# Delta rule inverse: substitution on 16-wide blocks only, larger blocks joined on TensorE in turn

## The chip, the cores and the metric

One Trainium2 chip, one NeuronCore of it. The metric is the device time of one execution in microseconds (us). All arithmetic is in 32-bit floats; the large projections split each operand into two rounded parts and take three products.

## The reference, cut to what matters

Two small model blocks run one after the other on a sequence of 512 tokens of width 1024. The second block's first mixer is a gated delta rule with 16 value heads of width 128, which this change touches:

```python
L = jnp.where(strict, jnp.einsum('bhncd,bhnsd->bhncs', kb, k) * decay, 0.0)
eye = jnp.eye(CHUNK, dtype=q.dtype)
T = lax.linalg.triangular_solve(eye + L, jnp.broadcast_to(eye, L.shape),
                                left_side=True, lower=True, unit_diagonal=True)
u = T @ vb
w = T @ (kb * jnp.exp(g)[..., None])
...
def step(state, inp):
    v_new = u_n - jnp.einsum('bhcd,bhde->bhce', w_n, state)
    o = (jnp.einsum('bhcd,bhde->bhce', q_n, state)
         + jnp.einsum('bhcs,bhse->bhce', a_n, v_new))
    state = state * gl_n[..., None, None] + jnp.einsum('bhcd,bhce->bhde', k_n, v_new)
```

T is the inverse of a unit lower triangular matrix, one for each head and chunk of tokens. The scan over chunks needs T of a chunk before it can go on.

## The kernel before

The kernel is one program written through a layer that traces every operation in program order, finds the dependencies, allots buffers of named tiles, and then orders each engine's instructions itself by a planner's cost model; it sets all semaphores. Each engine then works through its own list in that order. So the order of the trace is the planner's and not that of the source, and taking operations away may reorder others.

The delta rule is the function `gdn`. It works in chunks of 128 tokens, four of them, and on pairs of value heads (gi = 0 to 7) which share a key head; a pair has 8 matrices (2 heads x 4 chunks), numbered n.

- `stage_a(gi)` projects q and k (L1083), convolves and normalises them, makes the products k k and q k (L1099), multiplies them with masks and decays into `Am` (L1120, L1121, on VectorE) and `At` (L1122, on GpSimd, as are the products `qd` of L1126), and inverts.
- The inverse starts from the 32x32 diagonal blocks, 4 per matrix, 32 in all. They go through DRAM (`ad`, L1131 and L1135) into `ai`, so that each partition holds one whole block, four copies of it; partition group s then solves eight of its 32 columns, `ui`. L1138 loads unit columns. Substitution is row by row: the loop of L1140 to L1144 solves the two 16-wide halves of the block at once in 15 steps of a product and a sum; L1146 to L1149 take what the first half gives to the second; L1150 to L1153 solve the second half's rows for the first half's columns, 15 steps more. Each step needs the one before.
- The result goes back through DRAM (`ud`, L1156 and L1162) into `uc`, 32 rows of each block in 32 partitions; `tcp` is its transpose by 32x32 blocks (L1164).
- The join: 32-wide blocks are joined to 64 (L1177 to L1191) and 64 to 128 (L1192 to L1198) by two matrix products each, over the PSUM tile `mg`, of which there is one buffer. The first loop goes through the two 64-wide halves m one after the other, each with its eight matrices in a row, so that eight products in a row use the same 32x32 part of the array. ScalarE copies results to `z32`, `tz` and the result `U`.
- `stage_v` and `stage_z` project values and gates; `stage_b` is the scan over chunks, which reads `U` in L1243; `stage_g` normalises and gates; `stage_o` projects out, its sums evicted by VectorE in L1292.

The loop of L1297 emits, for each gi, `stage_v(gi + 1)`, `stage_a(gi + 2)`, `stage_b(gi)`, `stage_z(gi)`, `stage_g(gi)` and `stage_o(gi - 1)`, so a pair's inverse is emitted two iterations ahead of its use. Projections are in the helper `mm3` (L145 to L147); their weights are fetched on SP's queue (L138), rounded by ScalarE (L139) and their rests taken by VectorE (L140), in three buffers; their sums go to three PSUM banks `acc`.

Of the kernel before, what the change touches and what calls it, by code (L numbers as in the profile page):

```python
# [12 lines left out]
AF = mybir.ActivationFunctionType  # L13
ALU = mybir.AluOpType
AX = mybir.AxisListType
# [4 lines left out]
D, S, DFF, KT, P = 1024, 512, 2816, 8, 128  # L20
# [415 lines left out]
def fdims(t, off, *dims):  # L436

    return bass.AP(tensor=t.tensor, offset=t.offset + off, ap=[list(t.ap[0])] + [list(d) for d in dims])
# [528 lines left out]
def gdn(self, feed0, gate, tail):  # L967
    nc, tc, A = self.nc, self.tc, self.A
    with tc.tile_pool(name="gd", bufs=1) as gd, tc.tile_pool(name="gdd", bufs=1, space=bass.MemoryType.DRAM) as dr:
        def T(name, shape=(P, S), dtype=F32, bufs=None):  # L970
            return gd.tile(list(shape), dtype, name=name, bufs=bufs)
# [102 lines left out]
        def stage_a(gi):  # L1074
# [3 lines left out]
            for u in range(2):  # L1078
# [5 lines left out]
                x = T(f"x{u}", bufs=2 + u)  # L1084
# [3 lines left out]
            rb, r, pk = norms(qk, 1.0, "sa", gi < 2)  # L1088
# [5 lines left out]
            q, k = qk  # L1094
# [17 lines left out]
            Am, At = T("Am", (P, 8, P), bufs=2), T("At", (P, 8, P), bufs=2)  # L1112
            for a in range(2):
# [5 lines left out]
                m = Am[:, a * 4:(a + 1) * 4, :]  # L1119
# [6 lines left out]
                nc.gpsimd.tensor_mul(qd[:, a], q, gbc[:, a])  # L1126


            ad = dr.tile([8, 4, 32, 32], F32, name="ad", bufs=2)
            for b in range(4):  # L1130
                nc.sync.dma_start(ad[:, b].rearrange("n j i -> j n i"), Am[32 * b:32 * b + 32, :, 32 * b:32 * b + 32])  # L1131
            ai = T("big", (P, 32, 32), bufs=3)
# [4 lines left out]
            ui = T("ui", (P, 8, 32), bufs=2)  # L1137
            nc.sync.dma_start(ui, A["gdn_eye"])  # L1138
            mt = T("mt", (P, 2, 4, 16), bufs=2)
            for t in range(1, 16):  # L1140
# [2 lines left out]
                                     fdims(ai, t, (528, 2), (0, nq), (32, t + 1)))  # L1143
                nc.vector.tensor_reduce(fdims(ui, t, (144, 2), (32, nq), (1, 1)), mt[:, :, :nq, :t + 1], axis=AX.X,  # L1144
                                        op=ALU.add, negate=True)
            for v in range(2):  # L1146
                x = T("ix").rearrange("p (q i j) -> p q i j", q=4, i=8)
                nc.vector.tensor_mul(x, fdims(ui, 0, (32, 4), (0, 8), (1, 16)), fdims(ai, 16 + 8 * v, (0, 4), (1, 8), (32, 16)))
                nc.vector.tensor_reduce(ui[:, 0:4, 16 + 8 * v:24 + 8 * v], x, axis=AX.X, op=ALU.add, negate=True)  # L1149
            for t in range(1, 16):  # L1150
                nc.vector.tensor_mul(mt[:, 0, :, :t + 1], ui[:, 0:4, 16:17 + t],
                                     fdims(ai, 16 * 32 + 16 + t, (0, 4), (32, t + 1)))
                nc.vector.tensor_reduce(ui[:, 0:4, 16 + t:17 + t], mt[:, 0, :, :t + 1], axis=AX.X, op=ALU.add, negate=True)  # L1153
            ud = dr.tile([8, 4, 8, 4, 32], F32, name="ud", bufs=2)
            for s in range(4):
                nc.sync.dma_start(ud[:, :, :, s].rearrange("n b q i -> (n b) q i"), ui[32 * s:32 * s + 32])  # L1156
# [1 line left out]
            U = T("U", (P, 8, P), bufs=2)  # L1158
            nc.gpsimd.memset(U, 0.0)
            uc = T("uc", (P, 8, 32))  # L1160
            for b in range(4):
                nc.sync.dma_start(uc[32 * b:32 * b + 32], udv[b])  # L1162
            tcp = T("tcp", (P, 8, 32))
            nc.vector.transpose(tcp.rearrange("p n i -> p (n i)"), uc.rearrange("p n i -> p (n i)"))  # L1164
            lo, hi = slice(0, 64), slice(64, P)
            tz = T("tz", (P, 8, 64))
            t64, z64 = tz[lo], tz[hi]
            nc.gpsimd.memset(t64, 0.0)
            for b in range(4):
                sl = slice(32 * b, 32 * b + 32)  # L1170
                nc.scalar.copy(U[sl, :, sl], uc[sl])
                if b < 2:
                    nc.scalar.copy(t64[sl, :, sl], tcp[sl])
            n8 = "p (n i) -> p n i"
            z32 = T("z32", (P, 8, 32))
            pm = self.bank("mg")
            for m in range(2):  # L1177
                s0, s1 = slice(64 * m, 64 * m + 32), slice(64 * m + 32, 64 * m + 64)
                for n in range(8):
                    nc.tensor.matmul(pm[s1, n * 32:(n + 1) * 32], Am[s0, n, s1], tcp[s0, n, :], start=True, stop=True)  # L1180
                nc.scalar.copy(z32[s1], pm[s1, 0:256].rearrange(n8, n=8))
            for m in range(2):
                s0, s1 = slice(64 * m, 64 * m + 32), slice(64 * m + 32, 64 * m + 64)
                for n in range(8):
                    nc.tensor.matmul(pm[s0, n * 32:(n + 1) * 32], z32[s1, n, :], uc[s1, n, :], start=True, stop=True)  # L1185
                if m == 0:
                    for n in range(8):
                        nc.tensor.matmul(pm[s1, 256 + n * 32:256 + (n + 1) * 32], uc[s1, n, :], z32[s1, n, :],
                                         start=True, stop=True)
                    nc.scalar.activation(t64[s1, :, s0], pm[s1, 256:512].rearrange(n8, n=8), AF.Copy, scale=-1.0)  # L1190
                nc.scalar.activation(U[s0, :, s1], pm[s0, 0:256].rearrange(n8, n=8), AF.Copy, scale=-1.0)  # L1191
            pm = self.bank("mg")  # L1192
            for n in range(8):
# [99 lines left out]

        og, last = {}, []
        st = {gi: stage_a(gi) for gi in range(2)}
        vs = {0: stage_v(0)}
        for gi in range(8):  # L1297
            if gi < 7:
                vs[gi + 1] = stage_v(gi + 1)
            if gi < 6:  # L1300
                st[gi + 2] = stage_a(gi + 2)
            if gi == 0:
                self.late()
            oT = stage_b(gi, st.pop(gi), vs.pop(gi))
            z = stage_z(gi)
            og[gi] = stage_g(gi, oT, z)
            if gi:
                stage_o(gi - 1, og.pop(gi - 1))
# [436 lines left out]
```

## Time and profile before

| | us |
|---|---|
| median of 3 runs | 2827.94 (2823.83 to 2828.9) |
| the profiled execution | 2832.52 |
| its span | 2830.7 |
| TensorE (PE) busy in the span | 2718.2 |
| weight loads (PEld) | 2218.0 |
| VectorE (DVE) busy | 1774.8 |
| ScalarE (ACT) busy | 1194.0 |
| GpSimd (POOL) busy | 239.4 |

The delta rule lies between about 1860 and 2470 us of the span. A product of 32-bit floats shows as two MATMUL records, and the end of a record is modelled; the distance between starts says how fast they go. PEclk is the share of its full clock that TensorE was granted, over a stretch; SP is the engine that issues the DMAs.

### The profile page before, as it was taken

The page shows a single profiled execution, that of the slowest core. Times are in us where ns is not written, and L with a number is a line of the kernel's source. Part 1 is how long each engine was busy: PE and PEld are TensorE (multiplying, and loading weights), DVE is VectorE, ACT ScalarE, POOL GpSimd, SP SyncE. Part 2 cuts the span into 40 slices and gives each one's busy share as a digit, 9 for nine tenths or more (in the row PEclk, how much of TensorE's full clock was granted, in tenths as well). Part 3 has the DMA queues.
Part 4 walks back from the last instruction along what each step waited for, and adds up shares of the span by engine and source line. Part 5 has one row for each costly group of instructions (what it writes and reads, how often), then busy time and mean ns, then how long its engine had stood idle before and what let it go on. Part 6 is the DMA issues. An engine that isn't in the chain of part 4 may idle for free.

```text
span 2830.7 us, 36488 instructions
## 1 busy us (share of the span) xinstructions
PE 2718.2 (96%) x13879; PEld 2218.0 (78%) x13879; DVE 1774.8 (63%) x3321; ACT 1194.0 (42%) x2192; POOL 239.4 (8%) x224
## 2 busy tenths in 40 slices
PE   8999999999999999999899999988999999999998
PEld 6888878788888888887678888876777777777776
DVE  6454577754545644358854343599778788577765
ACT  4222254532323422233463232374545444477773
POOL 0000002000000000005310000030111111120001
PEclk9999999999999999999999999999889999899999
DMA  5343332244443433322113333323223233132221
GB/s 184 116 139 108 125 93 75 90 134 120 133 127 106 137 103 97 96 87 86 50 60 94 100 95 99 92 66 113 76 86 105 88 96 89 43 99 68 78 63 62
DMA packets 106704, 274.49 MB, mean 97 GB/s; under 512 B 35465, under 2 KB 39553, under 8 KB 106529
## 3 DMA queue, kind: packets, MB, share of 16 engines
q1 hardware_dynamic: 106528, 272.15, 31.3%
q8 instruction: 110, 1.80, 0.3%
q14 instruction: 66, 0.53, 0.1%
HBM read 267.79 MB, written 4.31 MB: 96 GB/s over the span
## 4 chain that ended last, share of the span: by engine, by line
PE 35%; DVE 10%; ACT 3%; issue 1%; POOL 1%; DMA 0%; DVEq 0%; SPq 0%; POOLq 0%; ACTq 0%
PE acc L145 9%; PE acc L146 9%; PE acc L147 9%; DVE wl L140 1%; PE mg L1484 1%; POOL x L1389 1%; DVE Am L1121 1%; DVE mt L1142 0%; PE sb L1475 0%; PE mg L1185 0%; DVE Am L1120 0%; ACT wh L139 0%; PE mg L1194 0%; PE sb L1254 0%; PE sb L1243 0%
## 5 line engine op out<-in xcount | busy, mean ns | idle before, releaser
L145 PE MATMUL acc<-xh,wh 128*128 128x512 f32 (+2 forms) x2320 | 914.5, 395 | 18.9 <-ACT xh L186 8.2
L146 PE MATMUL acc<-xl,wh 128*128 128x512 f32 (+1 forms) x2320 | 906.9, 391 | 5.4 <-POOL xl L151 3.2
L147 PE MATMUL acc<-xh,wl 128*128 128x512 f32 (+1 forms) x2320 | 903.3, 390 | 2.0 <-DVE wl L140 2.0
L139 ACT CAST wh<-raw 128x1024 fp32r<-128x1024 f32 (+3 forms) x430 | 439.3, 1022 | 1076.7 <-PE acc L146 713.3
L140 DVE TENSOR_TENSOR wl<-raw,wh 128x1024 fp32r<-128x1024 f32 (+2 forms) x410 | 488.1, 1192 | 97.0 <-ACT wh L139 93.2
L145 PEld LDWEIGHTS acc<-xh,wh 128*128 128x128 f32 (+1 forms) x2320 | 438.2, 189 | 110.5 <-ACT xh L186 8.2
L146 PEld LDWEIGHTS acc<-xl,wh 128*128 128x128 f32 x2320 | 438.2, 189 | 95.0 <-POOL xl L151 4.5
L147 PEld LDWEIGHTS acc<-xh,wl 128*128 128x128 f32 x2320 | 437.6, 189 | 92.4 <-DVE wl L140 3.5
L146 PE MATMUL acc<-al,wh 128*128 128x512 f32 (+1 forms) x720 | 278.1, 386 | 0.0
L147 PE MATMUL acc<-ah,wl 128*128 128x512 f32 (+1 forms) x720 | 277.8, 386 | 0.0
L145 PE MATMUL acc<-ah,wh 128*128 128x512 f32 (+1 forms) x720 | 277.4, 386 | 0.0
L249 DVE SCALAR_TENSOR_TENSOR h<-acc,h 128x512 f32<-128x512 f32 x128 | 88.4, 690 | 215.7 <-PE acc L147 215.3
L289 DVE TENSOR_TENSOR tmp<-acc,rstd 128x512 f32<-128x512 f32 x88 | 60.9, 691 | 240.0 <-PE acc L147 240.0
L287 DVE TENSOR_TENSOR tmp<-acc,rstd 128x512 f32<-128x512 f32 x88 | 60.8, 691 | 176.2 <-PE acc L147 176.1
L146 PEld LDWEIGHTS acc<-al,wh 128*128 128x128 f32 x720 | 135.2, 188 | 28.6 <-DVE al L151 0.8
L145 PEld LDWEIGHTS acc<-ah,wh 128*128 128x128 f32 x720 | 135.2, 188 | 28.2
L147 PEld LDWEIGHTS acc<-ah,wl 128*128 128x128 f32 x720 | 135.2, 188 | 28.0
L145 PE MATMUL acc<-ogh,wh 128*128 128x512 f32 (+1 forms) x256 | 111.5, 440 | 19.4 <-DVE h L1292 19.2
L140 POOL TENSOR_TENSOR wl<-raw,wh 128x1024 fp32r<-128x1024 f32 (+1 forms) x20 | 47.8, 2393 | 872.2 <-ACT wh L139 861.2
L146 PE MATMUL acc<-ogl,wh 128*128 128x512 f32 (+1 forms) x256 | 106.4, 416 | 0.0
L147 PE MATMUL acc<-ogh,wl 128*128 128x512 f32 (+1 forms) x256 | 105.0, 410 | 0.0
L150 ACT CAST ah<-tmp 128x512 fp32r<-128x512 f32 x88 | 54.8, 623 | 63.9 <-DVE tmp L290 63.9
(448 smaller groups left out, 3589.0 us busy)
## 6 DMA issues: line engine op xcount, KB each, us to landing
raw<-in_wi_dram SPq DMA_DIRECT2D x176, 512.0 KB
raw<-in_wo_dram SPq DMA_DIRECT2D x64, 512.0 KB
raw<-in_ada_w_dram SPq DMA_DIRECT2D x48, 512.0 KB
raw<-in_a_in_dram SPq DMA_DIRECT2D x48, 512.0 KB
raw<-in_b_in_dram SPq DMA_DIRECT2D x24, 512.0 KB
raw<-in_wo_dram SPq DMA_DIRECT2D x24, 384.0 KB
raw<-in_a_out_dram SPq DMA_DIRECT2D x16, 512.0 KB
big<-rd SPq DMA_DIRECT2D x13, 512.0 KB
```

The lines of the kernel that those rows point to most:

```text
L139: nc.scalar.copy(wh[:, :n], raw[:, :n])
L140: self.lo_eng.tensor_tensor(wl[:, :n], raw[:, :n], f32(wh[:, :n]), op=ALU.subtract)
L145: nc.tensor.matmul(out, ah, bh, start=start, stop=False)
L146: nc.tensor.matmul(out, ah, bl, start=False, stop=False)
L147: nc.tensor.matmul(out, al, bh, start=False, stop=stop)
L150: self.nc.scalar.copy(hi, x)
L249: nc.vector.scalar_tensor_tensor(self.h[m], ps, scale(m), self.h[m], op0=ALU.mult, op1=ALU.add)
L287: nc.vector.tensor_mul(t, pg, rstd)
L289: nc.vector.tensor_mul(u, pu, rstd)
L1121: nc.vector.tensor_mul(m, m, bcol[:, :, hs[a]:hs[a] + 1].to_broadcast([P, 4, P]))
L1389: nc.gpsimd.tensor_mul(x, x, r)
L1484: nc.tensor.matmul(po[pair[a], j * P:], vs[p][:, j, vo:vo + 64], pT[a][:, j, j * P:], start=j == 0, stop=j == 3)
```

## The change

The second half of the substitution (L1146 to L1153) is removed: `ui` then holds the inverses of the two 16x16 diagonal blocks of every 32x32 block and zeros between them. After `uc` is back and transposed, a new first join makes the 32-wide blocks: for each matrix n and each of its four blocks, a product of 16 rows of `Am` with `tcp`, a copy to `z32`, a product of `z32` with the upper 16 columns of `uc`, and a subtraction from `uc`; then `tcp` is made anew. The loops of the 32-to-64 join are turned inside out, so that for each matrix n the products of the two halves follow one another, and neighbouring products use different parts of the array. The join from 64 to 128 stays.

```diff
--- before.py
+++ after.py
@@ -1126,6 +1126,7 @@
                 nc.gpsimd.tensor_mul(qd[:, a], q, gbc[:, a])
 
 
+
             ad = dr.tile([8, 4, 32, 32], F32, name="ad", bufs=2)
             for b in range(4):
                 nc.sync.dma_start(ad[:, b].rearrange("n j i -> j n i"), Am[32 * b:32 * b + 32, :, 32 * b:32 * b + 32])
@@ -1143,14 +1144,6 @@
                                      fdims(ai, t, (528, 2), (0, nq), (32, t + 1)))
                 nc.vector.tensor_reduce(fdims(ui, t, (144, 2), (32, nq), (1, 1)), mt[:, :, :nq, :t + 1], axis=AX.X,
                                         op=ALU.add, negate=True)
-            for v in range(2):
-                x = T("ix").rearrange("p (q i j) -> p q i j", q=4, i=8)
-                nc.vector.tensor_mul(x, fdims(ui, 0, (32, 4), (0, 8), (1, 16)), fdims(ai, 16 + 8 * v, (0, 4), (1, 8), (32, 16)))
-                nc.vector.tensor_reduce(ui[:, 0:4, 16 + 8 * v:24 + 8 * v], x, axis=AX.X, op=ALU.add, negate=True)
-            for t in range(1, 16):
-                nc.vector.tensor_mul(mt[:, 0, :, :t + 1], ui[:, 0:4, 16:17 + t],
-                                     fdims(ai, 16 * 32 + 16 + t, (0, 4), (32, t + 1)))
-                nc.vector.tensor_reduce(ui[:, 0:4, 16 + t:17 + t], mt[:, 0, :, :t + 1], axis=AX.X, op=ALU.add, negate=True)
             ud = dr.tile([8, 4, 8, 4, 32], F32, name="ud", bufs=2)
             for s in range(4):
                 nc.sync.dma_start(ud[:, :, :, s].rearrange("n b q i -> (n b) q i"), ui[32 * s:32 * s + 32])
@@ -1160,34 +1153,50 @@
             uc = T("uc", (P, 8, 32))
             for b in range(4):
                 nc.sync.dma_start(uc[32 * b:32 * b + 32], udv[b])
-            tcp = T("tcp", (P, 8, 32))
-            nc.vector.transpose(tcp.rearrange("p n i -> p (n i)"), uc.rearrange("p n i -> p (n i)"))
+            n8 = "p (n i) -> p n i"
+            z32, tcp = T("z32", (P, 8, 32)), T("tcp", (P, 8, 32))
+
+            def turned():
+                nc.vector.transpose(tcp.rearrange("p n i -> p (n i)"), uc.rearrange("p n i -> p (n i)"))
+            quart = [slice(32 * b, 32 * b + 32) for b in range(4)]
+
+            turned()
+            pm = self.bank("mg")
+            for n in range(8):
+                for q in quart:
+                    r = slice(q.start, q.start + 16)
+                    nc.tensor.matmul(pm[q, n * 32:(n + 1) * 32], Am[r, n, q], tcp[r, n, :], start=True, stop=True)
+            nc.scalar.copy(z32, pm[:, 0:256].rearrange(n8, n=8))
+            for n in range(8):
+                for q in quart:
+                    nc.tensor.matmul(pm[q, 256 + n * 16:256 + (n + 1) * 16], z32[q, n, :], uc[q, n, 16:32], start=True,
+                                     stop=True)
+            nc.vector.tensor_sub(uc[:, :, 16:32], uc[:, :, 16:32], pm[:, 256:384].rearrange(n8, n=8))
+            turned()
             lo, hi = slice(0, 64), slice(64, P)
             tz = T("tz", (P, 8, 64))
             t64, z64 = tz[lo], tz[hi]
             nc.gpsimd.memset(t64, 0.0)
-            for b in range(4):
-                sl = slice(32 * b, 32 * b + 32)
-                nc.scalar.copy(U[sl, :, sl], uc[sl])
+            for b, q in enumerate(quart):
+                nc.scalar.copy(U[q, :, q], uc[q])
                 if b < 2:
-                    nc.scalar.copy(t64[sl, :, sl], tcp[sl])
-            n8 = "p (n i) -> p n i"
-            z32 = T("z32", (P, 8, 32))
+                    nc.scalar.copy(t64[q, :, q], tcp[q])
             pm = self.bank("mg")
-            for m in range(2):
-                s0, s1 = slice(64 * m, 64 * m + 32), slice(64 * m + 32, 64 * m + 64)
-                for n in range(8):
+            both = ((quart[0], quart[1]), (quart[2], quart[3]))
+            for n in range(8):
+                for s0, s1 in both:
                     nc.tensor.matmul(pm[s1, n * 32:(n + 1) * 32], Am[s0, n, s1], tcp[s0, n, :], start=True, stop=True)
+            for s0, s1 in both:
                 nc.scalar.copy(z32[s1], pm[s1, 0:256].rearrange(n8, n=8))
-            for m in range(2):
-                s0, s1 = slice(64 * m, 64 * m + 32), slice(64 * m + 32, 64 * m + 64)
-                for n in range(8):
+            for n in range(8):
+                for s0, s1 in both:
                     nc.tensor.matmul(pm[s0, n * 32:(n + 1) * 32], z32[s1, n, :], uc[s1, n, :], start=True, stop=True)
-                if m == 0:
-                    for n in range(8):
-                        nc.tensor.matmul(pm[s1, 256 + n * 32:256 + (n + 1) * 32], uc[s1, n, :], z32[s1, n, :],
-                                         start=True, stop=True)
-                    nc.scalar.activation(t64[s1, :, s0], pm[s1, 256:512].rearrange(n8, n=8), AF.Copy, scale=-1.0)
+            s0, s1 = both[0]
+            for n in range(8):
+                nc.tensor.matmul(pm[s1, 256 + n * 32:256 + (n + 1) * 32], uc[s1, n, :], z32[s1, n, :], start=True,
+                                 stop=True)
+            nc.scalar.activation(t64[s1, :, s0], pm[s1, 256:512].rearrange(n8, n=8), AF.Copy, scale=-1.0)
+            for s0, s1 in both:
                 nc.scalar.activation(U[s0, :, s1], pm[s0, 0:256].rearrange(n8, n=8), AF.Copy, scale=-1.0)
             pm = self.bank("mg")
             for n in range(8):
```

## Rows read from the trace of the kernel before

**Rows 1.** Page: busy us, share of the span and instructions of each engine.

```profile
PE 2718.2 (96%) x13879; PEld 2218.0 (78%) x13879; DVE 1774.8 (63%) x3321; ACT 1194.0 (42%) x2192; POOL 239.4 (8%) x224
```

**Rows 2.** Windows: start:end length, PE PEld DVE ACT POOL busy, PEclk, DMA, GB/s.

```profile
1860.00:2100.00 240.00, 216.17 (x1313) 176.55 (x1312) 194.39 (x488) 125.58 (x315) 39.26 (x40) 0.88 0.32 93
2100.00:2410.00 310.00, 289.44 (x1796) 231.28 (x1795) 257.11 (x673) 149.35 (x410) 43.05 (x39) 0.96 0.31 92
2410.00:2470.00 60.00, 53.43 (x340) 44.29 (x339) 29.61 (x73) 21.74 (x61) 5.62 (x8) 0.80 0.17 50
```

**Rows 3.** Waits of TensorE, 1860 to 2470: total us, times, longest.

```profile
PE acc L145 <- DVE h L1292: 19.2, 5, 6.1
...
PE mg L1180 <- DVE mt L1142: 3.0, 1, 3.0
...
PE mg L1180 <- DVE nr L1047: 2.4, 1, 2.4
```

**Rows 4.** Groups by line, VectorE, 1860 to 2470: count, busy us, mean ns, idle before.

```profile
L1151 DVE TENSOR_TENSOR mt<-ui,big 128x8 f32<-128x8 f32 (+14 forms) x120 | 28.2, 235 | 0.7
...
L1153 DVE TENSOR_REDUCE ui<-mt 128x4 f32<-128x8 f32 (+14 forms) x120 | 22.2, 185 | 0.7
...
L1148 DVE TENSOR_TENSOR ix<-ui,big 128x512 f32<-128x512 f32 x16 | 17.3, 1080 | 0.0
...
L1149 DVE TENSOR_REDUCE ui<-ix 128x32 f32<-128x512 f32 x16 | 11.0, 685 | 0.0
...
L1259 DVE SCALAR_TENSOR_TENSOR St<-St,egl,sb 128x128 f32<-128x128 f32 x32 | 10.6, 342 | 5.8 <-PE sb L1254 5.6
...
L1164 DVE STREAM_TRANSPOSE tcp<-uc 128x256 f32<-128x256 f32 x8 | 3.5, 440 | 1.3 <-DMA uc<-ud 1.2
```

**Rows 5.** Timeline: start us, duration us; second pair's first use of U, last pair's chain.

```profile
2032.48 0.58 PE L1243 MATMUL sb<-vnat,U 128*128 128x128 f32 x1 [0.68 <-ACT U L1198]
...
2387.77 1.13 DVE L1148 TENSOR_TENSOR ix<-ui,big 128x512 f32<-128x512 f32 x1
...
2408.13 0.22 DVE L1153 TENSOR_REDUCE ui<-mt 128x4 f32<-128x64 f32 x1
...
2433.84 0.59 ACT L1198 ACTIVATE U<-mg 64x512 f32<-64x512 f32 x1 [3.32 <-PE mg L1197]
...
2435.60 1.06 PE L1243 MATMUL sb<-vnat,U 128*128 128x128 f32 x4
```

**Rows 6.** Group by line, ScalarE, same stretch.

```profile
L1181 ACT COPY z<-mg 32x256 f32<-32x256 f32 x16 | 5.8, 365 | 10.2 <-PE mg L1180 10.1
```

**Rows 7.** Timeline of TensorE around a join of the first pair.

```profile
1979.84 0.47 PE L145 MATMUL acc<-xh,wh 128*128 128x512 f32 x1
1980.24 0.69 PE L1180 MATMUL mg<-tcp,Am 32*32 32x32 f32 x16
1980.86 0.50 PE L146 MATMUL acc<-xl,wh 128*128 128x512 f32 x1
1981.20 0.40 PE L147 MATMUL acc<-xh,wl 128*128 128x512 f32 x1
1981.43 0.39 PE L145 MATMUL acc<-xh,wh 128*128 128x512 f32 x1
```

**Rows 8.** Timeline of TensorE in the first mixer, four tiles in turn.

```profile
421.12 0.45 PE L620 MATMUL sa<-lx 64*32 64x32 f32 x32
```

**Rows 9.** Windows over three joins.

```profile
2020.00:2040.00 20.00, 18.01 (x131) 14.62 (x130) 13.81 (x50) 10.04 (x30) 1.17 (x2) 0.50 0.08 28
2070.00:2090.00 20.00, 19.00 (x136) 14.30 (x137) 9.19 (x27) 7.47 (x15) 0.52 (x1) 0.51 0.25 80
2150.00:2160.00 10.00, 10.00 (x107) 8.01 (x106) 3.88 (x7) 5.16 (x9) 0.52 (x1) 1.00 0.48 165
```

**Rows 10.** Timeline of a regular iteration: Am on VectorE, the projection that waits.

```profile
2272.70 3.42 DVE L1121 TENSOR_TENSOR Am<-Am,gbcol 128x512 f32<-128x512 f32 x2
...
2277.98 0.79 PE L145 MATMUL acc<-ogh,wh 128*128 128x512 f32 x1 [6.14 <-DVE h L1292]
```

## The prediction

> **What bounds the kernel now.** I read four views in this order: the page's busy times, the windows over the stage that the diff touches, the waits of TensorE in that stage, and the groups of instructions by line. On the page the reader is to see that TensorE is busy 96% of the span and VectorE 63% [rows 1]. In the windows over that stage, 1860 to 2470 us, TensorE stands idle 24 of the first 240 us, 21 of the next 310 and 7 of the last 60, and its mean clock is 0.88, 0.96 and 0.80 [rows 2]. The clock has two levels, 1.2 and 2.4 GHz, so these means are (1 - 0.88) x 2 x 240 = 58 us, 25 us and 24 us at the half level. So the stage is bound by TensorE for most of its time, and loses time in two ways: gaps, and stretches at half clock behind them. The waits say who makes the gaps: VectorE, 19.2 us for the evictions of L1292, and 3.0 and 2.4 us for what L1180 needs before the join [rows 3]. VectorE works on long chains of short instructions there. Whatever the change brings must come out of these 51 us of gaps and the 53 us that half clock costs; the busy time that VectorE loses counts for nothing by itself.
>
> **What it removes.** L1148, L1149, L1151 and L1153, 16 + 16 + 120 + 120 instructions: 17.3 + 11.0 + 28.2 + 22.2 = 78.7 us of VectorE, 9.8 us for each of the eight head pairs [rows 4]. Being one dependent chain between other work, it takes longer than its sum: for the last pair it begins at 2387.8 and ends at 2408.4, 20.6 us [rows 5]. That much earlier the inverse U can be ready.
>
> **What it adds, on VectorE and ScalarE.** A second 32x32 block transpose (0.44 us, L1164) and a subtraction of 128x128 elements from PSUM; nearest row L1259, same shape and source, 0.34 us [rows 4]. That is 0.78 us a pair, 6 us in all, against 78.7 removed. One more copy of 256 elements per partition on ScalarE, as L1181's 0.37 us [rows 6]: 3 us, on an engine busy 297 of 610 us [rows 2]. Both lie beside TensorE's projections (L145 to L147) and I cost them at nothing as work; should that cover be missing, as at the end of the stage, they are 1.2 us a pair. As waits they return below. The four copies into U (L1171) now come after the subtraction; they are off TensorE's path until U is joined. No DMA is added or removed. Each pair's eight through DRAM (L1156, L1162) are only due earlier on SP's queue, past fetches of weights (L138) that must wait for a buffer in any case; POOL's queue issues the same memsets. I cost this at 0; 3 us either way would bound it.
>
> **What it adds on TensorE.** Two groups of 32 products a pair, each product two records in the trace, so 64 records a group. The price of a record: L1180 now gives 16 records to one tile in 0.69 us, of which the last takes 0.19 by itself, so 33 ns each; with the two projections that follow, the group sets TensorE back from 1979.84 to 1981.20, 1.36 us, where two projection steps take 0.46 (the next one is 0.23): 0.90 us, 0.53 of records and 0.37 of switching [rows 7]. Where four tiles are issued in turn the trace has a row as well, in the first mixer: 32 records of L620 in 0.45 us, the last again 0.19 of it, 8 ns each [rows 8]. The new groups name four tiles in turn, so I take 8 ns: 64 x 8 ns = 0.51, + 0.37 = 0.88 us a group, 1.76 a pair. The old joins, now in turn over two tiles at 16 ns, go from two groups of 0.90 to one of 0.51 + 0.37: 0.92 saved on L1180, about as much on L1185. Sum: 1.76 - 1.8 = 0, 0 us over eight pairs. Bounds: below, the second group streams 16 columns instead of 32, at best half the records' time, -0.26 a pair or -2 us; above, no gain from turns, 2 x (64 x 33 ns + 0.37) - 2 x 0.37 = +4.2 a pair, +34 us.
> In L620 the row groups that run together write different banks of PSUM; the new groups write one bank, and no row here shows that. The Trainium skill, page "TensorEngine Tiling (Array Packing)", section "Gotcha 1: PSUM Pressure", says that different row tiles cannot use the same PSUM bank at a time. By it the groups would go product by product, at the upper bound; without it, at mine. The new products also lie in different columns and so in different partitions of the bank, which is why I keep the 8 ns.
>
> **What lies on the path.**
> (a) The second and third pairs. The first products of a chunk with U (L1243) wait directly for U at 2032.48 [rows 5], and 2020 to 2040 and 2070 to 2090 run at a clock of 0.50 and 0.51, with TensorE busy 18.0 and 19.0 us; the same joins at 2150 run at 1.00 [rows 9]. What they did before differs: at the slow ones TensorE had just waited 3.0 and 2.4 us for VectorE at L1180 [rows 3]. The half clock costs (18.0 + 19.0) / 2 = 18.5 us, gaps 5.4 and 3.0: 27 us. Freed of 10 us of work per pair, VectorE should come to the transpose in time; but TensorE's projections remain, and the new join asks VectorE again in mid-join. Bounds 0 and -27; I take just under half, -12.
> (b) The regular iterations. TensorE's waits for L1292, 19.2 us, come behind the scaling of Am (L1121, 3.42 us for two while POOL multiplies): the projection at 2277.98 waited 6.14 us [rows 10]. None of that is removed and I take 0 (bounds 0 to -19).
> (c) The end. The last U is ready at 2434.4 and its first use is at 2435.6 [rows 5], so nothing covers its chain. It comes 20.6 us earlier, less the new join: two groups 1.76, the copy 0.37, subtraction and transpose 0.78 and hand-overs, some 3.6 us: 17 us. But TensorE, in the last 60 us, has only 6.6 us of idle and 24 / 2 = 12 of half clock to give back [rows 2], 18.6 at the utmost. I take -11 (bounds 0 and -17).
> (d) The new wait. TensorE goes in order: the old join (L1180) now waits for the new products, a copy, products, a subtraction and a transpose, and so twice on the queue of VectorE, and behind it stand projections, whose banks and weight buffers VectorE's evictions and ScalarE's casts wait for. On VectorE, the evictions L1292 and the splits L140 stand behind the subtraction. The nearest price is the wait that L1180 has now: 5.4 us over eight pairs [rows 3]. I take the same again, +5; bounds 0, and 3 us in every pair with a stretch of 18 us at half clock, 9 us more: 12 a pair, +96.
>
> Sum: -12 + 0 - 11 + 5 + 0 = -18 us. The profiled execution took 2832.5 us (2830.7 of span and 1.8 around it), so 2814.5; it lies 4.6 above the median of 2827.9. On the median's scale the forecast is **2810 us**.
>
> **Rivals.** One, more than forecast: with VectorE less laden, the evictions are no longer late either. Then the 19.2 us of waits go and, of the middle's 25 us at half clock, 8 of the 12 that they cost: 2810 - 27 = 2783. For it: VectorE is busy 257 of those 310 us [rows 2]. Against: what the evictions wait for stays. Chance 0.14.
> Two, nothing: U comes earlier but TensorE has its projections to do in any case, (a) gives nothing, and of (c) only the 5 us stay that (d) takes back: 2828. For it: TensorE is busy 216 of the first 240 us. Chance 0.16.
> Three, the other side by turns that don't overlap: the tiles that share a bank go one after another, and the groups cost +34 us in a stage that TensorE bounds: 2810 + 34 = 2844. It would decide from 22 ns a record on: 2 x 64 x 14 ns x 8 pairs are 14 us, with the two-tile groups' share 18. This is what the rule of the Trainium skill quoted above would do. Against: L620's turns at 8 ns. Chance 0.10.
> Four, slower by the new wait: the join, now earlier, falls where VectorE has evictions, Am and POOL's multiplications at once, TensorE stands 3 us in mid-join, and the small products behind it run at half clock, 12 us a pair. In four of eight pairs that is +48 less the -23 of (a) and (c): 2827.9 + 25 = 2853. It decides from two pairs on. For it: L1180 waits so in two of eight pairs today. Against: in the other six it doesn't. Chance 0.18.
> That the substitution is removed but its time stays on VectorE I hold excluded.
>
> **How the numbers follow.** The forecast's own case has 0.42, range 2798 to 2822. A difference under 0.2%, 5.7 us, cannot be told from none. Faster: the first rival's 0.14, 0.39 of the forecast's and 0.04 of the second's, 0.57. Same: 0.03 of the forecast's, 0.11 of the second's and 0.02 of the third's, 0.16. Slower: the rest, 0.27. The range of 2778 to 2845 holds the first rival, the second and most of the third, and leaves out most of the fourth.
>
> **What would show it.** Right: L1148 to L1153 gone and L1142 to the write of ud directly behind it; the records of the new groups 8 ns apart; the last U some 15 us before its stage ends now, and 2020 to 2090 at full clock. Wrong: new records 30 ns apart (third rival); TensorE waiting for the subtraction or second transpose by more than 5 us in all, or more than 107 us at half clock (fourth); waits for L1292 under 10 us (first).

## The result and the profile after

The changed kernel takes 2783.11 us (median of 4 runs, 2782.95 to 2784.58) against 2826.49: a ratio of 0.9848, interval 0.9831 to 0.9865, 43.4 us less. The forecast was 18 less.

The page, beside [rows 1]: TensorE (PE) is busy 34 us less although it has 1024 records more, VectorE (DVE) 45 us less. I had 73 less, from the durations of [rows 4]; but the records of VectorE overlap their neighbours, which the page counts once (below, the same steps put back measure 53 in the stage).

```profile
PE 2684.0 (97%) x14903; PEld 2192.8 (79%) x14903; DVE 1729.3 (62%) x3065; ACT 1194.4 (43%) x2200; POOL 240.4 (9%) x224
```

The same windows as in [rows 2] (start:end length, busy time and count of PE, PEld, DVE, ACT, POOL, then PEclk, DMA, GB/s). The clock is now 0.95 and 0.99 instead of 0.88 and 0.96, and the middle window has 12 us of gaps instead of 21. The third window already holds the start of the next mixer.

```profile
1860.00:2100.00 240.00, 217.94 (x1834) 178.13 (x1833) 190.22 (x432) 133.61 (x347) 39.84 (x41) 0.95 0.34 98
2100.00:2410.00 310.00, 298.27 (x2537) 240.35 (x2532) 230.94 (x508) 156.98 (x423) 42.18 (x39) 0.99 0.32 93
2410.00:2470.00 60.00, 52.75 (x376) 47.00 (x375) 49.18 (x94) 38.59 (x81) 18.64 (x27) 0.94 0.26 81
```

TensorE's waits in the same stretch, beside [rows 3]: those for the evictions (L1292, now L1301) are 6.7 us instead of 19.2, and no join waits for VectorE any more. L1220 waits for VectorE's convolution (L1016).

```profile
PE sb L1220 <- DVE cv L1016: 8.4, 5, 5.0
PE acc L145 <- DVE h L1301: 6.7, 8, 2.4
```

TensorE's timeline around a new join (start, duration): the 64 records of the first group (L1168) take 0.75 us, those of the second (L1172) 0.72. With the last record's 0.19 us taken off, that is 9 ns a record. This stands against the 33 ns of [rows 7].

```profile
2163.48 0.38 PE L1247 MATMUL sb<-St,x 128*128 128x128 f32 x2
2163.79 0.75 PE L1168 MATMUL mg<-tcp,Am 16*32 16x32 f32 x64
2164.47 0.49 PE L1247 MATMUL sb<-St,x 128*128 128x128 f32 x2
...
2165.36 0.72 PE L1172 MATMUL mg<-uc,z 32*32 32x16 f32 x64
```

The last pair, beside [rows 5]: the substitution ends at 2346.8, U's last part is copied at 2372.6, and U is first used at 2384.4. U now lies ready 11 us ahead of its first use, where it was 1.2 us. Measured from the end of the stage, U is 15 us earlier (87.6 us ahead of the next mixer's first statistic instead of 72.4), as forecast.

```profile
2346.48 0.28 DVE L1145 TENSOR_REDUCE ui<-mt 128x8 f32<-128x128 f32 x1
...
2372.60 0.59 ACT L1207 ACTIVATE U<-mg 64x512 f32<-64x512 f32 x1 [1.21 <-PE mg L1206]
...
2384.37 0.61 PE L1252 MATMUL sb<-vnat,U 128*128 128x128 f32 x4
```

**A ledger of the stage.** I cut the stage at its first product (L1002, a transpose of the decays) and at the first statistic of the next mixer, and inside it at the first product that uses U, in the first, fourth and seventh pair. In each part I count TensorE's gaps, the loss to the half clock (half of the busy time in stretches granted 0.5), and what is left, TensorE's own time at full clock. The letters are the prediction's. In us, from the two profiled executions:

| | before | after |
|---|---|---|
| stage | 620.8 | 577.5 |
| gaps | 52.9 | 37.8 |
| loss to half clock | 48.3 | 13.4 |
| own time | 519.6 | 526.3 |
| gaps + half clock: ahead of the first pair | 16.9 | 17.3 |
| first to fourth pair, (a) | 32.8 | 14.4 |
| fourth to seventh, (b) | 24.7 | 8.9 |
| seventh to the end, (c) | 26.9 | 10.6 |

The stage is 43.3 us shorter, as much as the medians differ. The two profiled executions differ by 6 us more, which lie outside the stage; that of before was 6 above its median, so the ledger is uncertain by some such amount.

Own time can be checked against runs below that give TensorE the same products. The kernel before and four variants of it with its joins have 519.5 to 525.1 us (mean 522.6), four with the old join in turn and no new join 509.8 to 511.4 (510.5), the changed kernel and five variants of it 521.6 to 528.7 (524.5).

### The profile page after: what moved, and what is told of

Same layout as the page of the kernel before. It is cut to its first block, busy times and chain, and to the rows that moved or that the text cites. A ratio compares the mean times of both kernels' runs of the same rounds, so it can differ in the third digit from the quotient of the medians.

```text
span 2781.3 us, 38312 instructions
## 1 busy us (share of the span) xinstructions
PE 2684.0 (97%) x14903; PEld 2192.8 (79%) x14903; DVE 1729.3 (62%) x3065; ACT 1194.4 (43%) x2200; POOL 240.4 (9%) x224
## 5 line engine op out<-in xcount | busy, mean ns | idle before, releaser
L145 PE MATMUL acc<-ogh,wh 128*128 128x512 f32 (+1 forms) x256 | 105.0, 412 | 10.5 <-DVE h L1301 6.7
L146 PE MATMUL acc<-ogl,wh 128*128 128x512 f32 (+1 forms) x256 | 100.0, 391 | 0.0
```

What stands on the lines that cost most here:

```text
L145: nc.tensor.matmul(out, ah, bh, start=start, stop=False)
L146: nc.tensor.matmul(out, ah, bl, start=False, stop=False)
```

## The experiments

All ratios are to the kernel before on the same chip. The expectations weigh four theories of the gain: A, VectorE's lighter load; B, the old join's turns; C, the shorter chain to U; D, that GpSimd's multiplications no longer fall beside VectorE's scaling of `Am`.

**Turns alone.** Only the old join's loops are turned in the kernel before.

```diff
-            for m in range(2):
-                s0, s1 = ...
-                for n in range(8):
+            for n in range(8):
+                for s0, s1 in both:
                     nc.tensor.matmul(pm[s1, ...], Am[s0, n, s1], tcp[s0, n, :], ...)
```

> The kernel before, whole substitution kept, with only the loops of the 32-to-64 join turned inside out, so that neighbouring products use different parts of the array. Theory A (the gain is VectorE's: its 9.8 us a pair of short instructions stood beside the scaling of Am and the evictions): turning saves 0.9 us on each of two groups, 1.8 us a pair, 14 us at the very most and some 5 when part of it was slack, so 2814 to 2828 on the scale of 2826.5, and the waits for the evictions of L1292 stay near 19 us. Rival B (the turns do most of it, by fewer stretches at half clock behind the joins): 2800 or less, and the half clock in the stage falls by more than 40 us. Rival C (the shorter chain to U) expects the same as theory A.

2797.4 us, ratio 0.9898 (0.9881 to 0.9914): 28.8 us, rival B's number. But the busy time of the two turned groups falls by 13 us only. It is 25.3 us in the kernel before (groups by line in the stage: count, busy us, mean ns, idle before),

```profile
L1185 PE MATMUL mg<-uc,z 32*32 32x32 f32 x256 | 13.2, 209 | 0.5 <-ACT z L1181 0.5
L1180 PE MATMUL mg<-tcp,Am 32*32 32x32 f32 x256 | 12.1, 201 | 7.3 <-DVE mt L1142 3.0 <-DVE nr L1047 2.4 <-ACT z L1181 1.8
```

and 12.2 us with turns:

```profile
L1186 PE MATMUL mg<-uc,z 32*32 32x32 f32 x256 | 6.3, 204 | 2.5 <-ACT z L1183 2.5
...
L1181 PE MATMUL mg<-tcp,Am 32*32 32x32 f32 x256 | 5.9, 198 | 5.5 <-DVE tcp L1164 5.5
```

In the ledger own time falls by 9.8 us, loss to half clock by 14.1, gaps by 2.5. So half of the gain is half clock.

**Tile by tile.** The kernel after, both joins' loops with the tile outside.

```diff
-            for n in range(8):
-                for q in quart:
+            for q in quart:
+                for n in range(8):
```

> The kernel after, with the products of the first two joins issued tile by tile (eight in a row to one part of the array) instead of in turn. By the prices of before, 33 ns a record against 8, each of the two new groups of 64 records grows by 1.6 us (the second, with 16 columns, by 1.2 or more) and the old joins by 0.9 each: 4 to 5 us a pair, 32 to 40 us in all if TensorE has no slack, so 2815 to 2823. If the old joins cost the same either way and the new products have slack: 2790 to 2800. If turns are worth nothing: 2783. Theory A and rival C both expect 2805 to 2823, and the waits for the evictions of L1301 still under 10 us.

2828.7 us, ratio 0.9997 (0.9984 to 1.0011), so 45.6 above the kernel after, more than either theory gave. The groups tell the direct part: 64 records take 1.91 and 2.38 us where they took 0.75 and 0.72.

```profile
2183.87 1.91 PE L1168 MATMUL mg<-tcp,Am 16*32 16x32 f32 x64
...
2186.60 2.38 PE L1172 MATMUL mg<-uc,z 32*32 32x16 f32 x64
```

The first group takes 27 ns a record; the second runs partly at half clock (0.72 granted on average). In the profiled execution (2820.3 us) own time is up by 21.5 us, half clock by 14.5, and gaps are not up. TensorE and VectorE work through the tiles in the same order here as in the kernel after, so this price, unlike most below, holds no change of order.

**Load put back.** The removed steps are put back into the kernel after, as work that nobody reads; the planner lets the transposes go ahead of them.

```diff
+            dx = T("dx", (P, 4, 32))
+            for v in range(2):
+                ...
+                nc.vector.tensor_reduce(dx[:, 0:4, 16 + 8 * v:24 + 8 * v], x, ...)
+            for t in range(1, 16):
+                ...
             ud = dr.tile([8, 4, 8, 4, 32], F32, name="ud", bufs=2)
```

> The kernel after, with the removed VectorE steps put back as work whose result goes to a scratch tile that nobody reads: the load of 9.8 us a pair is there again, the chain from the first substitution to U is not longer, since the transposes go ahead of the dead steps. Theory A (load): most of the gain goes, 2810 to 2828, and TensorE's waits for the evictions of L1301 (L1310 here) go back from 6.7 to over 15 us. Rival C (the chain to U): the gain stays, 2783 to 2790, waits for evictions under 10 us. Rival D (the planner's order moved POOL's multiplications off the scaling of Am): by which order comes out here; if the scaling runs clear of POOL, 2783 to 2790.

2792.8 us, 0.9883 (0.9868 to 0.9897): 9.6 of the 43 us come back, and the waits for evictions are 10.1 us. Theory A as the main cause falls.

**GpSimd's multiplications on VectorE**, first in the kernel before, then in the kernel after.

```diff
-                nc.gpsimd.tensor_mul(At[:, ...], qkm, e)
+                nc.vector.tensor_mul(At[:, ...], qkm, e)
...
-                nc.gpsimd.tensor_mul(qd[:, a], q, gbc[:, a])
+                nc.vector.tensor_mul(qd[:, a], q, gbc[:, a])
```

> The kernel before, with the multiplications of At and qd on VectorE instead of GpSimd, so that nothing of GpSimd runs beside the scaling of Am. VectorE gets 4 more instructions a pair, by the 0.68 us that the scaling takes undisturbed about 2.7 us a pair or 22 us in all. Rival D (before, it was the collision of POOL's multiplications with the scaling of Am, 3.42 us for two instead of 1.4, that made the evictions late): the waits for L1292 fall from 19 to under 8 us, their half clock goes with them, 15 to 25 us gained: 2802 to 2812. Theory A (VectorE's load): the load is greater, no gain or a loss, 2826 to 2840, waits for L1292 of 19 us or more. Rival C: 2826, no change.

> The kernel after, with the multiplications of At and qd on VectorE instead of GpSimd. In the kernel before this gave 14.6 us, with the waits for L1292 at 5.0 instead of 19.2. Theory D (the change already took the scaling of Am out of POOL's way): nothing left to win, waits for L1301 stay near 6.7, VectorE has 20 us more to do: 2780 to 2792. Against it (the two gains add up, since POOL's multiplications still slow some VectorE instruction twofold, now L1284 and the normalisations): 2765 to 2778.

Before: 2812.7 us, 0.9947 (0.9932 to 0.9963). After: 2769.2, 0.9806 (0.9791 to 0.9821). The gains are 14.6 and 13.9 us: they add up, so the collisions as a whole cost both kernels alike and are not what the change removed. They show in VectorE's groups. In the kernel before one scaling of `Am` takes 1288 ns on average,

```profile
L1121 DVE TENSOR_TENSOR Am<-Am,gbcol 128x512 f32<-128x512 f32 x16 | 20.4, 1288 | 0.0
```

and 685 ns with GpSimd idle beside it, where the work that came from GpSimd takes as long:

```profile
L1121 DVE TENSOR_TENSOR Am<-Am,gbcol 128x512 f32<-128x512 f32 x16 | 11.0, 685 | 0.0
L1122 DVE TENSOR_TENSOR At<-gt,tmp 128x512 f32<-128x512 f32 x16 | 10.9, 686 | 2.7 <-PE sb L1254 2.7
```

On GpSimd the same 16 instructions took 26.9 us. In the kernel after, the collisions have moved rather than gone: the scaling of `Am` meets fewer of them, and the gating of the scan's output (`oT`) meets more (10 instructions of over 1 us for 2).

```profile
L1121 DVE TENSOR_TENSOR Am<-Am,gbcol 128x512 f32<-128x512 f32 x16 | 14.1, 886 | 0.1
```

**A longer chain.** In the kernel after, the substitution's result goes through DRAM and back, four times or once.

```diff
+            for r in range(4):
+                hop = dr.tile([P, 256], F32, name="hop", bufs=2)
+                nc.sync.dma_start(hop, ui...)
+                nc.sync.dma_start(ui..., hop)
             ud = dr.tile([8, 4, 8, 4, 32], F32, name="ud", bufs=2)
```

> The kernel after, with the result of the first substitution sent through DRAM and back four times before it goes on: no work is added to any engine but the 8 DMAs of 128 KB on SP's queue, and the chain from the substitution to U is longer by some 16 to 20 us, an estimate from the 20.6 us that the removed steps took. After the runs so far: turning alone gave 28.8 of the gain (2797.4), the load of the removed steps put back beside the chain took only 9.6 back (2792.8). Theory C (what is left of the gain comes from U being ready earlier: the scan's first pairs and the end of the stage don't wait): most of the last pair's gain goes and part of the second and third pairs', 2798 to 2815. Theory A (load alone): 2781 to 2788.

> The kernel after, with one trip of the substitution's result through DRAM instead of four; by the run with four a trip puts some 4.9 us on the chain, and the four cost 32 us. If each microsecond of the chain costs alike: a quarter, 8 us, 2789 to 2793. If the loss begins only when the chain has eaten up some slack: 2783 to 2786.

Four trips: 2815.1 us, 0.9964 (0.9947 to 0.9982), theory C at its upper end. The last U is again ready only 1.2 us ahead of its use, and part (c) of the ledger is 25.8 us instead of 10.6. One trip: 2772.0, 0.9813 (0.9792 to 0.9834), faster than without it by 11 us, which no theory had. With one trip the fourth to seventh pair have 0.7 us of gaps instead of 8.9, with the same products. The trace shows TensorE's and VectorE's instructions in another order. That the order brings the gain is argued, not shown; if it does, an order is worth as much as the effects I was comparing.

**The new products twice**, and **no new join**.

```diff
-            for n in range(8):
+            for n in range(16):
+                n = n % 8
                 for q in quart:
```

> The kernel after, with each of the two groups of new products issued twice (the second pass writes the same values again). The price of the new products by itself: if a record is 8 ns, 64 records a group are 0.51 us and the repeated pass adds 1.0 us a pair without any switching, 8 us in all: 2788 to 2794. If the ledger of the traces (16 us for the new products, 2.06 a pair with their switching) is all records: 2796 to 2802. If the join is off TensorE's path: 2781 to 2785.

Twice: 2827.5 us, 1.0014 (1.0003 to 1.0026), 44 us more than the kernel after and outside every expectation. The second passes are cheap, +5 us of own time, but in all eight pairs TensorE stood still in the second group: its waits (total us, times, longest) show "issue", which means that it waited for nothing that the profile shows.

```profile
PE mg L1174 <- issue: 12.3, 8, 1.7
```

In the timeline of one pair 128 records of the first group and 100 of the second go at full pace, and then TensorE stands 1.39 us. More half clock goes with it (29 us in the ledger instead of 13).

```profile
2181.70 1.29 PE L1169 MATMUL mg<-tcp,Am 16*32 16x32 f32 x128
...
2183.50 1.03 PE L1174 MATMUL mg<-uc,z 32*32 32x16 f32 x100
2185.91 0.43 PE L1174 MATMUL mg<-uc,z 32*32 32x16 f32 x28 [1.39 <-issue]
```

What it may have waited for shows among the DMA queues, between 2183 and 2186 us (packets, MB, share): one transfer of instructions, begun at 2183.5.

```profile
q8 instruction: 1, 0.02, 2.0%
```

All eleven waits of TensorE with "issue" in this stage end 2.3 to 2.8 us after such a transfer began, where this queue has 44 transfers in the stage. So I take it that TensorE waited for its own instructions; no run changed that alone.

No new join:

```diff
-            turned()
-            pm = self.bank("mg")
-            ...
-            nc.vector.tensor_sub(uc[:, :, 16:32], uc[:, :, 16:32], pm[:, 256:384]...)
             turned()
```

> The kernel after without the new 16-to-32 join: both groups of its products, the copy, the subtraction and the first of the two transposes are left out, so the corners of the 32-wide blocks stay zero. It prices the new join as a whole. By the forecast's terms, 14.1 us of TensorE (1.76 a pair) and a wait of 5: 2764 to 2769. By the ledger of the traces, 16.5 us: 2767. If it also brings half clock or waits, as the doubled products did (44 us for 8 of records): below 2760. If it is hidden: 2781 to 2785.

2775.6 us, 0.9824 (0.9800 to 0.9848): the new join costs 7.5 us by the medians, but the intervals of the two kernels overlap. Own time falls by 16.1, but gaps and half clock rise by 8.6. This run and the other three below without the new join leave the corners of the 32-wide blocks zero, so they do not compute the inverse and serve as prices only.

**The old join undone** in the kernel after (the first diff backwards).

> The kernel after, with only the 32-to-64 join issued as in the kernel before, tile by tile and one half after the other; the new 16-to-32 products stay in turn. Issuing both joins tile by tile cost 45.6 us, and turning the old one alone gave the kernel before 28.8. If the old join is what counts, through the half clock behind its long runs on one tile: 2803 to 2814, half clock in the stage up by over 15 us. If a join is worth what its records are (0.9 us on each of two groups, 1.8 a pair): 2795 to 2800. If the new products in turn take over its part: 2783 to 2790.

2795.0 us, 0.9911 (0.9885 to 0.9937): 11.9 more by the medians, 18 by the ratios. The turns that won 28.8 in the kernel before are worth 12 to 18 here. (The execution with the profile took 2809.3 us, with a stretch of 24 us at half clock after one join, and raises the ratio; I draw nothing from its trace.)

**A version that is faster**: the third group in turn too, then with GpSimd's multiplications on VectorE.

```diff
             for n in range(8):
                 nc.tensor.matmul(pm[s1, 256 + ...], uc[s1, n, :], z32[s1, n, :], ...)
+                for s2, s3 in both:
+                    nc.tensor.matmul(pm[s2, ...], z32[s3, n, :], uc[s3, n, :], ...)
```

> The kernel after, with the third group of the 32-to-64 join (eight products that still use one tile) issued in turn with the second group, three products at a time. Each of its 16 records costs 33 ns now; in turn with the others about 11, so 0.35 us a pair, and without a group of its own another 0.37 of switching: 3 to 6 us in all, 2777 to 2780. If runs on one tile are also followed by half clock here, as in the old join: down to 2772. If it lies in slack: 2783.

> The same, and the multiplications of At and qd on VectorE as well, which gave 14.6 us on the kernel before and 13.9 on the kernel after. If the two add up: 2763 to 2767; if the second gain is the same time as the first: 2769.

The third group in turn: 2780.9 us, 0.9846 (0.9826 to 0.9866), not told from the kernel after. With both: 2761.6, 0.9781 (0.9758 to 0.9803), the fastest, 21.5 us under the kernel after.

**Order against edit.** The last six runs take the change apart, four of them with another order in the source. "Exchanged" means:

```diff
-            if gi < 7:
-                vs[gi + 1] = stage_v(gi + 1)
             if gi < 6:
                 st[gi + 2] = stage_a(gi + 2)
+            if gi < 7:
+                vs[gi + 1] = stage_v(gi + 1)
```

> The kernel before, with the same work and the same joins, but each pair's stage_a emitted ahead of the next pair's stage_v instead of behind it, so that the planner puts the projections, the inverse and the evictions in another order. It tells how much an order alone moves the time. If the order is worth little: 2821 to 2832. If it is worth what the one trip gave, 11 us or more, either way: under 2818 or over 2836.

> The same exchange of stage_a and stage_v in the kernel after. If the order is worth little: 2778 to 2788. If it is worth 11 us or more either way: under 2773 or over 2794; then no single edit's effect below some 11 us can be told from that of the order it brings.

> The kernel before without the second half of the substitution, the join tile by tile as it was, and no new join: the corners of the 32-wide blocks stay zero. With turns the removal without the new join took the time from 2797.4 to 2775.6, 21.8 us. If removal and turns add up: 2803 to 2807. If they win the same half clock twice, as undoing the old join's turns in the kernel after suggests (11.9 instead of 28.8): 2784 to 2792. The forecast's terms (a) and (c) without the new join: 2826.5 - 23 = 2803.

> The kernel after without the new join (2775.6), and with the removed VectorE steps put back as work that nobody reads. Beside the kernel before with turns (2797.4), which has the same load on VectorE and the same products on TensorE, it has only the shorter chain to U. If VectorE's load is what the removal won (theory A): 2793 to 2799. If it is the chain (theory C): 2774 to 2780. With 9.6, as in the kernel after: 2785.

> The kernel before with the old join in turn and with stage_a emitted ahead of stage_v. In the first order the turns won 28.8 us, of which the traces show 9.8 as TensorE's own time and the rest as gaps and half clock; in the second order the kernel before takes 2806.1. If the turns' own part is what always comes and the rest hangs on the order: 2794 to 2799. If the turns win their 28.8 in any order: 2777. If order and turns win the same time: 2803 to 2808.

> The kernel before without the second half of the substitution and without a new join, and with stage_a emitted ahead of stage_v. In the first order this removal won 52 us (2775.0). If it wins 52 in any order: 2754. If it reaches a floor of the stage, whatever the order: 2770 to 2780. If the order costs here what it cost the kernel after (12.6): 2785 to 2790.

| ratio to the kernel before (us) | order as it was | exchanged |
|---|---|---|
| kernel before | 1 (2826.5) | 0.9931, 0.9916 to 0.9946 (2806.1) |
| turns alone | 0.9898 (2797.4) | 0.9895, 0.9877 to 0.9912 (2795.4) |
| removal alone, no new join | 0.9817, 0.9803 to 0.9832 (2775.0) | 0.9930, 0.9904 to 0.9957 (2805.6) |
| the change | 0.9848 (2783.1) | 0.9887, 0.9870 to 0.9904 (2795.8) |

Down the first column the turns win 29 us, the removal 52, the change 43. Down the second they win 10, 0 and 12 (differences of the ratios; each uncertain by 6 to 9). Turns and removal together, without the new join, are no better than removal alone (2775.6). So the turns' own time, some 10 us, comes in both orders; the removal's 52 came in one.

The exchange is no neutral shuffle, however: it also has each inverse done earlier. In the kernel before, the second to seventh U lie ready 0.1 to 18.5 us ahead of their first use, and TensorE waits for the second [rows 5]. Exchanged, they lie ready 28 to 64 us ahead; the second pair:

```profile
2021.61 0.59 ACT L1198 ACTIVATE U<-mg 64x512 f32<-64x512 f32 x1 [0.66 <-PE mg L1197]
...
2050.59 0.38 PE L1243 MATMUL sb<-vnat,U 128*128 128x128 f32 x1
```

There a shorter chain can win directly only at the last pair, whose U is ready 0.3 us ahead of its use. The removal alone does win 8 us in part (c) there, and loses 9 in (a) and (b) together. So a part of the removal's gain in the first column may be the chain, at the second pair. For (b) that is less likely, since U lay ready 11 us and more ahead there even before the change.

With the load alone put back on the run without the new join: 2783.3 us, 0.9848 (0.9833 to 0.9863), between the theories. By the medians 7.7 us of the removal are load (53 us of VectorE's busy time in the stage, 491 for 438), which is not clear of the noise. The other 14.1, by which this run beats the turns alone, are the chain or the order that each edit brings.

TensorE's waits say why no single one of them carries the gain. In the order as it was, the evictions of stage_o are late. With the load alone back (L1298),

```profile
PE acc L145 <- DVE h L1298: 24.3, 5, 5.6
```

without load and new join (L1289),

```profile
PE acc L145 <- DVE h L1289: 15.6, 5, 5.8
```

and with removal alone (L1284), from the same load on VectorE as the one just shown:

```profile
PE acc L145 <- DVE h L1284: 4.9, 5, 2.0
```

So neither the load nor the chain alone sets these waits. In the exchanged order TensorE waits elsewhere: for VectorE's convolution and normalisation, and for ScalarE's rounding of the gated output. In the kernel before

```profile
PE sa L1036 <- DVE x L1016: 10.7, 6, 4.0
PE acc L145 <- ACT ogh L150: 6.2, 2, 5.7
PE sb L1061 <- DVE nr L1050: 6.2, 2, 5.0
```

and in the changed one, where the forecast's new wait also appears (L1168 for the transpose L1160):

```profile
PE sb L1061 <- DVE nr L1050: 13.0, 4, 4.0
PE sa L1036 <- DVE x L1016: 6.8, 2, 4.3
PE mg L1168 <- DVE tcp L1160: 4.2, 3, 3.6
```

## Why the forecast was wrong

**The products, 0 us: right in mechanism and nearly in size.** New products 14.1 forecast, 16.1 of own time measured (the run without the new join); turned join -14.4 forecast, -9.8 measured. Net +6.7 in the ledger of the change; over all runs with the same products it is 14 and -12, net +2. The third rival, tiles that share a bank going one after another, is out: four tiles in one bank go at 9 ns a record, and at 27 when issued tile by tile. By the Trainium skill, page "TensorEngine Tiling (Array Packing)", section "Gotcha 1: PSUM Pressure", different row tiles cannot access one bank at a time; the 9 ns of this trace show no such cost for tiles that also differ in columns.

**(d), the new wait, +5: not in this order.** No join waits for VectorE, where it was 5.4 us [rows 3]. In the exchanged order the wait is there, 4.2 us. The fourth rival is out in both.

**(c), the end, -11: measured -16.3.** The mechanism showed, with U 15 us earlier, and gave more. In the exchanged order it is -8.1 (18.9 to 10.8), with the last U ready 20 us ahead of its use instead of 0.3. This is the term that came in both.

**(a), -12: measured -18.4**, inside its bounds, and +3.1 in the exchanged order (24.5 to 27.6), where the second to fourth U lie ready 28 us and more ahead of their use.

**(b), the step that failed: "None of that is removed and I take 0".** Measured: -15.8, with the waits for evictions at 6.7 us. What the step put the waits down to, the scaling of `Am` beside GpSimd, was in part removed after all: L1121 takes 886 ns on average for 1288, though the edit leaves the scaling and GpSimd's work as they were. That does not settle the waits either, since with the removal alone L1121 takes 1079 ns and the waits are 4.9 us. The first rival had this result with a chance of 0.14, and its 2783 is the measured time. That is luck: its reason, the lighter load, is not what the runs show, as the waits stay at 15.6 us without the load and the load put back costs 8 to 10 us. In the exchanged order (b) gives -3.6 (23.8 to 20.2).

Of the 25 us between forecast and result, (b) is 16, (a) 6, (c) 5 and (d) 5, less 7 for the products. So (b), and (a) with it, failed in this: I read gaps and half clock, 101 us of the stage, off one order, and asked which of them the removed instructions touch. What the runs showed in its place: the planner lays out the stage anew for almost any edit, and an exchange in the source alone moved the kernel before by 20 us down and the kernel after by 11 up, one trip through DRAM by 11 down. Of the change's 43 us some 12 come in either order, about what the turns alone give in the exchanged one. Some 31 come in the order as it was only; how much of that is the planner's accident and how much the chain, which the exchange had already eased, no run separates. In the exchanged order a forecast of 18 would have been nearer. Stage windows (columns as above, PEclk third from the end) of the kernel before in the exchanged order,

```profile
1883.40:2487.00 603.60, 549.78 (x3505) 446.04 (x3506) 490.38 (x1248) 303.55 (x806) 92.05 (x94) 0.95 0.29 89
```

and of the changed one,

```profile
1884.00:2474.40 590.40, 546.20 (x4529) 444.44 (x4530) 442.45 (x992) 304.93 (x814) 87.52 (x94) 0.95 0.31 91
```

show it in two numbers: 54 and 44 us of gaps, and the same clock of 0.95, where the order as it was had 53 and 38, and over its stage a clock of 0.91 that became 0.97. The half clock makes most of the difference: its loss goes from 25 us to 25 exchanged, and from 48 to 13 in the order as it was.

What stays open: which feature of the order makes it good or bad. Collisions of GpSimd with VectorE are worth 14 us, in both kernels alike; what the rest hangs on, no run singled out, and so the cause of (b) stays open. Two orders are also a small sample.

## What to carry to other kernels

Where a planner orders the instructions, forecast an edit's own time and the gaps apart. The first can be counted from rows (here to within 7 us); the second is a range as wide as what other orders of the same work give, and one exchange in the source gives a first sample of it. Credit an edit only with what it wins in more than one order, and look at what an exchange does to the chain that the edit shortens. Issue small products in turn over tiles: here that was three times as fast as tile by tile. Where two engines multiply side by side, try putting the work on one.

## What the runs showed that was not expected

- TensorE can stand still with no engine to wait for: in two doubled bursts of small products it stood 1.3 to 1.7 us, in eight pairs of eight, after 131 to 254 records, each time 2.3 to 2.8 us behind the start of an instruction transfer. 5 us more of own time cost 44.
- Four 32-wide tiles in turn, all in one PSUM bank: 9 ns a record, 27 tile by tile; two tiles in turn 16 (the 32 records of L1188 in 0.69 us, the last of it 0.19).
- VectorE's scaling of 128x512 elements takes 685 ns with GpSimd's multiplications gone, and 1288 on average (678 to 1780) with them; moved to VectorE, GpSimd's products for `At`, of the same size, take 686 ns instead of 1699.
- The loss to half clock (48 us before, 13 after, 6 in the fastest) follows the order too: the kernel before in the exchanged order, with the same products, had 25.
